# Hybrid four-mixer trunk: projection matmuls put in unbroken runs of 4096 columns

## The chip, the cores and the metric

The kernel runs on one core of one Trainium2 chip. The time is that of the device, from the start of the program to its end, in microseconds (us). PE is TensorE (PEld its weight loads), DVE VectorE, ACT ScalarE, POOL GpSimd, SP SyncE, from whose queue the DMAs here are issued.

## The reference

One decoder layer, float32, 2048 tokens of width 1024, then a final RMSNorm. One input projection (1024 to 9,232 columns) feeds four token mixers and their gates; each mixer's output goes through a SiLU gate path and its own projection, the four are merged by sigmoid gates, and one output projection closes the layer:

```python
h = rmsnorm(x, norm_g)
u = h @ w_in                       # split into the mixers' inputs, gate paths, merge gates
y_a = rg_lru(conv(lru_x)) * silu(lru_z)
y_b = (layernorm(sigmoid(m_o) * mlstm(q, k, v, i, f)) + skip * xm) * silu(m_z)
y_c = rmsnorm(gla(silu(h_q), hk, h_i, log_fh)) * silu(h_z)
y_d = rmsnorm(gla(g_q, g_k, g_v, log_gk)) * silu(g_z)
merged = sum(sigmoid(merge_n) * (y_n @ w_branch_n) for n in "abcd")
x = x + merged @ w_out
out = rmsnorm(x, final_g)
```

mLSTM, HGRN2 (`y_c`) and GLA (`y_d`) are recurrences over chunks of positions: within a chunk small products of queries, keys and values, between chunks a state that is decayed and added to.

## The kernel before

The sequence is worked in two halves of 1024 tokens, one after the other. Each half has these stages:

- **Ahead** (`ahead_pairs`, `ip_pair`): most of the input projection in seven products per pair of tiles (Strassen), with the LRU and the gate paths beside it. Its matmuls have line L423. 70 to 746 us and 1420 to 2097 us.
- **Mixers** (`mixers`): the mLSTM (`mlstm`, a generator), then four HGRN2 heads and two tiles with two GLA heads each, every one in two groups of 512 tokens (`gla_tile`, also a generator; 12 tiles per half). `both` steps the mLSTM beside the tiles. Between them stand projections that no mixer waits for at once: the values of the next heads (`ip_vals`, `ip_tok`, `tok_mm`: L280) and the last merge gates (`gate`, `ip_ch`, `proj_ch`: L268).
- **Merge** (`merge`): four branches of eight tiles, each tile two outputs of 512 tokens from 12 matmuls (`proj_ch`, L268). It starts while the last mixer tiles are still worked on; weights, gates and partial sums come and go by DMA.
- **Output** (`outp`): the output projection (`ip_tok`, `ip_tok_k`: L280) and the final norm.

Every projection is made of three matmuls per block of 128 inputs, since weights and activations are split into a high and a low part (`fp32r`): high by high, high by low, low by high. One output tile of `proj_ch` takes 24 matmuls of 512 columns (12 in the merge), one of `tok_mm` 24 of 256 or 264 columns. `wpieces` loads a block of weights (SP), casts it (ACT, L249) and forms the low part (POOL, L250). Projections write the PSUM banks `pb`, the recurrences the banks `mx`.

In a GLA tile, L997 and L1040 are the score products of 32 and 64 columns, at five levels; L1062 transposes the keys, L1068 forms the state's increments, which DVE turns into states at L1075, and L1083 and L1084 are the outputs. ACT squares and sums them (L1094), takes the logarithm and the exponential (L227, L1096) and scales them (L1102), PE transposes the result (L1106), and DVE multiplies it by the gate (L1107). In the mLSTM, L867 to L923 are its products and L945 a transpose. In the merge, ACT applies a tanh to the gates of the last two branches (L1313), and DVE multiplies by it out of PSUM (L1323); L1296 and L1297 split a branch's input.

The order on each engine is not written by hand. The framework's scheduler places instructions on all engines against a clock of its own; among those that are ready, the one with the smaller priority number goes first. Numbers count up in the order in which the code issues, and `prio(off)` lowers them for a block:

```python
p0 = tc.cur_priority
tc.cur_priority = max(0, p0 - off)
...
tc.cur_priority = p0 + (tc.cur_priority - s)
```

The mixers stand in `prio(MIX)` with `MIX = 4000`, evacuations and weight splits in `prio(EV)` with `EV = 6000`; the projections between them have no lowering. So a recurrence's matmul goes before a projection's as soon as it is ready, also in the middle of a projection's 24 matmuls. On the chip each engine keeps the order that the scheduler gave it.

Of the kernel before, what the change touches and what calls it, by code (L numbers as in the profile page):

```python
# [147 lines left out]
class Trunk:  # L148
# [90 lines left out]
    def wpieces(self, aps):  # L239
        nc = self.nc  # L240
        r = []
        with self.prio(self.EV):
            for ap in aps:
# [8 lines left out]
        return r  # L252

    EV = 6000

    def proj_ch(self, pieces, rh, rl, sink, ns=(0, 1)):


        nc = self.nc
        nk = 4 * len(pieces)  # L260
        for n in ns:
            ts = slice(n * 512, (n + 1) * 512)
            ps = self.pbank()
            for k in range(nk):
                hi, lo = pieces[k // 4]
                ws = slice((k % 4) * 128, (k % 4 + 1) * 128)
                for i, (w, h) in enumerate(((hi, rh[k]), (hi, rl[k]), (lo, rh[k]))):
                    nc.tensor.matmul(ps, w[:, ws], h[:, ts], start=(k == 0 and i == 0), stop=(k == nk - 1 and i == 2))  # L268
            sink(ts, ps)

    def ip_ch(self, name, j, sink, ns=(0, 1)):
# [3 lines left out]
    def tok_mm(self, v, c, k, pieces, ncol, first, last):  # L275
        hi, lo = pieces[k // 2]
        ws = slice((k % 2) * ncol, (k % 2 + 1) * ncol)
        cs = slice(c * 128, (c + 1) * 128)
        for i, (w, h) in enumerate(((hi, self.hh[k]), (lo, self.hh[k]), (hi, self.hl[k]))):
            self.nc.tensor.matmul(v, h[:, cs], w[:, ws], start=(first and i == 0), stop=(last and i == 2))  # L280

    def ip_tok(self, pieces, ncol, evac, single=8):

# [34 lines left out]
    def load_first(self, xs):  # L318
# [28 lines left out]
        for i, t in enumerate(tiles):  # L347
# [3 lines left out]
            def sink(ts, ps):  # L351
                with self.prio(self.EV):
                    V.tensor_tensor(th, ps, rb[:, :512], op=ALU.mult)
# [31 lines left out]
    def restore_block(self):  # L385

        nc = self.nc
        with self.prio(self.EV):
            for k in range(4):
# [10 lines left out]
    def ip_pair(self, t0, t1, fin, first=False):  # L400
# [4 lines left out]
        wc = self.a["wc"]  # L405
        with self.prio(self.EV):
            b11, b12, b22 = (r[:, :512] for r in self.wr)
# [4 lines left out]
        def product(x, w):  # L412
            with self.prio(self.EV):
                i = self.wi
                self.wi += 1
                hi, lo = self.wh[i % NW][:, :512], self.wl[i % NW][:, :512]
                A.activation(hi, w, AF.Copy)  # L417
                G.tensor_tensor(lo, w, hi, op=ALU.subtract)  # L418
            ps = self.bank8()
            for k, (xh, xl) in enumerate(self.op[x]):  # L420
                ws = slice(k * 128, (k + 1) * 128)
                for i, (wp, xp) in enumerate(((hi, xh), (hi, xl), (lo, xh))):
                    nc.tensor.matmul(ps, wp[:, ws], xp, start=(k == 0 and i == 0), stop=(k == 3 and i == 2))  # L423
            return ps

        def wsum(o, x, y):
            with self.prio(self.EV):
                V.tensor_tensor(o, x, y, op=ALU.subtract)  # L428
# [1124 lines left out]
```

## Time and profile before

| | us |
|---|---|
| median of 3 runs | 2724.45 (2722.39 to 2729.04) |
| the profiled execution | 2719.25 |
| its span, first to last instruction | 2717.4 |
| PE busy | 2596.0 |
| DVE, POOL, ACT busy | 1745.0, 1505.9, 1287.6 |

The profile shows one execution. Busy times are those of instructions on an engine, and a busy PE is not PE at its peak, since its matmuls overlap. "Clock" is the share of full speed that was granted to TensorE. A wait is idle time of an engine just before an instruction, put down to what ended it. In timelines, "x8" counts records, of which a float32 matmul has two and a transpose or an fp32r matmul one.

### The profile page before, as it was taken

How to read it: one execution, taken by the hardware profiler on the slowest of the kernel's cores; microseconds unless marked ns; L12 is line 12 of the kernel's file. 1: busy time of each engine (PE TensorE's matmuls, PEld its weight loads, DVE VectorE, ACT ScalarE, POOL GpSimd, SP SyncE). 2: the span in 40 equal slices, each digit the busy share in tenths (PEclk: the TensorE clock that was granted, in tenths of full speed). 3: DMA queues.
4: the chain of work that ended last, by engine and by line, in shares of the span. 5: the costliest groups of instructions: out<-in, count | busy, mean ns of one | idle time of the engine just before them, and what ended most of it. 6: DMA issues, size and time to landing. Idle time of an engine off the chain costs nothing. (4 is left out here: it accounts for less than half of the span.)

```text
span 2717.4 us, 45785 instructions
## 1 busy us (share of the span) xinstructions
PE 2596.0 (96%) x16800; PEld 2150.4 (79%) x16800; DVE 1745.0 (64%) x2907; ACT 1287.6 (47%) x2763; POOL 1505.9 (55%) x1273
## 2 busy tenths in 40 slices
PE   7999999999989998999999999999999999989999
PEld 5777878877878886778977777888787888767789
DVE  8787667447576778543375967764566677776342
ACT  5455444434454564443464454453345455644433
POOL 5566556444555555566475566554444555554763
PEclk8999999999999999999999999999999999999999
DMA  6233223443454336785442432233436533458821
GB/s 229 71 125 108 84 85 131 133 142 101 159 177 119 117 120 218 256 295 155 155 140 82 139 107 92 83 132 116 136 126 190 155 110 110 157 186 312 267 93 75
DMA packets 227072, 393.03 MB, mean 145 GB/s; under 512 B 20720, under 2 KB 78080, under 8 KB 226848
## 3 DMA queue, kind: packets, MB, share of 16 engines
q1 hardware_dynamic: 219360, 384.87, 42.9%
q10 hardware_dynamic: 7488, 5.24, 0.7%
q8 instruction: 132, 2.16, 0.3%
q14 instruction: 92, 0.75, 0.1%
HBM read 270.42 MB, written 119.60 MB: 144 GB/s over the span
## 5 line engine op out<-in xcount | busy, mean ns | idle before, releaser
L418 POOL TENSOR_TENSOR wl<-wr,wh 128x512 fp32r<-128x512 f32 x264 | 370.4, 1408 | 298.8 <-ACT wh L417 290.7
L418 POOL TENSOR_TENSOR wl<-gth,wh 128x512 fp32r<-128x512 f32 x198 | 286.9, 1449 | 280.1 <-ACT wh L417 268.6
L423 PE MATMUL mx<-s,wh 128*128 128x512 f32 x1248 | 394.0, 395 | 5.5 <-DVE arena L432 2.4
L432 DVE TENSOR_TENSOR arena<-arena,mx 128x512 f32<-128x512 f32 x386 | 252.3, 680 | 184.9 <-PE mx L423 168.3
L250 POOL TENSOR_TENSOR wl<-wr,wh 128x512 fp32r<-128x512 f32 (+1 forms) x176 | 249.1, 1423 | 179.3 <-ACT wh L249 144.9
L423 PE MATMUL mx<-hh,wl 128*128 128x512 f32 x824 | 328.6, 399 | 9.4 <-POOL wl L418 9.4
L423 PE MATMUL mx<-hh,wh 128*128 128x512 f32 x824 | 327.1, 397 | 5.6 <-DVE mqk L624 3.5
L423 PE MATMUL mx<-hl,wh 128*128 128x512 f32 x824 | 327.7, 398 | 2.3 <-DVE hl L306 2.3
L268 PE MATMUL pb<-hh,wh 128*128 128x512 f32 x704 | 289.2, 412 | 11.3 <-ACT hh L1296 3.4
L268 PE MATMUL pb<-hl,wh 128*128 128x512 f32 x704 | 287.2, 408 | 5.1 <-DVE hl L1297 5.1
L423 PEld LDWEIGHTS mx<-s,wh 128*128 128x128 f32 x1248 | 235.3, 189 | 62.4 <-DVE arena L432 2.8
L268 PE MATMUL pb<-hh,wl 128*128 128x512 f32 x704 | 284.1, 404 | 0.0
L417 ACT ACTIVATE wh<-wr 128x512 fp32r<-128x512 f32 x264 | 164.2, 627 | 227.3 <-PE mx L423 139.8
L280 PE MATMUL pb<-wh,hh 128*128 128x256 f32 (+1 forms) x880 | 255.3, 291 | 1.8 <-DVE lrt L1129 1.1
L280 PE MATMUL pb<-wl,hh 128*128 128x256 f32 (+1 forms) x880 | 254.5, 289 | 1.7 <-POOL wl L250 1.7
L280 PE MATMUL pb<-wh,hl 128*128 128x256 f32 (+1 forms) x880 | 253.5, 288 | 0.0
L423 PE MATMUL mx<-s,wl 128*128 128x512 f32 x624 | 245.0, 396 | 0.0
L417 ACT ACTIVATE wh<-gth 128x512 fp32r<-128x512 f32 x198 | 124.2, 627 | 228.9 <-DVE gth L428 185.5
L249 ACT ACTIVATE wh<-wr 128x512 fp32r<-128x512 f32 (+1 forms) x176 | 110.1, 629 | 187.1 <-PE pb L268 115.6
L423 PEld LDWEIGHTS mx<-hh,wl 128*128 128x128 f32 x824 | 156.2, 190 | 51.6 <-POOL wl L418 16.0
L423 PEld LDWEIGHTS mx<-hh,wh 128*128 128x128 f32 x824 | 156.5, 190 | 46.0 <-issue 6.9
L423 PEld LDWEIGHTS mx<-hl,wh 128*128 128x128 f32 x824 | 156.0, 189 | 41.0 <-DVE hl L306 3.5
(614 smaller groups left out, 6075.1 us busy)
## 6 DMA issues: line engine op xcount, KB each, us to landing
wr<-in_wc_dram SPq DMA_DIRECT2D x246, 256.0 KB, 2.7
g<-arena SPq DMA_DIRECT2D x52, 512.0 KB, 3.3
gth<-in_wc_dram SPq DMA_DIRECT2D x66, 256.0 KB, 2.8
wr<-in_wb_dram SPq DMA_DIRECT2D x64, 256.0 KB, 3.3
hl<-y SPq DMA_DIRECT2D x32, 512.0 KB, 5.8
arena<-g SPq DMA_DIRECT2D x48, 256.0 KB, 3.9
arena<-in_xT_dram SPq DMA_DIRECT2D x32, 256.0 KB, 4.7
lw<-g SPq DMA_DIRECT2D x32, 256.0 KB, 3.6
```

What stands on the lines that cost most here:

```text
L249: nc.scalar.activation(hi, raw, AF.Copy)
L250: nc.gpsimd.tensor_tensor(lo, raw, hi, op=ALU.subtract)
L268: nc.tensor.matmul(ps, w[:, ws], h[:, ts], start=(k == 0 and i == 0), stop=(k == nk - 1 and i == 2))
L280: self.nc.tensor.matmul(v, h[:, cs], w[:, ws], start=(first and i == 0), stop=(last and i == 2))
L417: A.activation(hi, w, AF.Copy)
L418: G.tensor_tensor(lo, w, hi, op=ALU.subtract)
L423: nc.tensor.matmul(ps, wp[:, ws], xp, start=(k == 0 and i == 0), stop=(k == 3 and i == 2))
L432: V.tensor_tensor(o, x, y, op=ALU.add)
```

## The change

Inside the loops of `proj_ch` and `tok_mm`, each matmul now stands in `run(i, n)`, with its number `i` in its output tile and its `n` columns. Where `i * n` is a multiple of 4096 the priority stays as it was; everywhere else it is lowered by 9000, more than the mixers' 4000. So the scheduler may put a recurrence's matmul ahead of a run's first matmul, and no longer ahead of the others: a run is 8 matmuls of 512 columns or 16 of 256. What is computed does not change.

```diff
--- before.py
+++ after.py
@@ -252,6 +252,16 @@
         return r
 
     EV = 6000
+    RUN = 9000
+
+    @contextmanager
+    def run(self, i, n):
+
+        if i * n % 4096:
+            with self.prio(self.RUN):
+                yield
+        else:
+            yield
 
     def proj_ch(self, pieces, rh, rl, sink, ns=(0, 1)):
 
@@ -265,7 +275,8 @@
                 hi, lo = pieces[k // 4]
                 ws = slice((k % 4) * 128, (k % 4 + 1) * 128)
                 for i, (w, h) in enumerate(((hi, rh[k]), (hi, rl[k]), (lo, rh[k]))):
-                    nc.tensor.matmul(ps, w[:, ws], h[:, ts], start=(k == 0 and i == 0), stop=(k == nk - 1 and i == 2))
+                    with self.run(3 * k + i, 512):
+                        nc.tensor.matmul(ps, w[:, ws], h[:, ts], start=(k == 0 and i == 0), stop=(k == nk - 1 and i == 2))
             sink(ts, ps)
 
     def ip_ch(self, name, j, sink, ns=(0, 1)):
@@ -277,7 +288,8 @@
         ws = slice((k % 2) * ncol, (k % 2 + 1) * ncol)
         cs = slice(c * 128, (c + 1) * 128)
         for i, (w, h) in enumerate(((hi, self.hh[k]), (lo, self.hh[k]), (hi, self.hl[k]))):
-            self.nc.tensor.matmul(v, h[:, cs], w[:, ws], start=(first and i == 0), stop=(last and i == 2))
+            with self.run(3 * k + i, 256):
+                self.nc.tensor.matmul(v, h[:, cs], w[:, ws], start=(first and i == 0), stop=(last and i == 2))
 
     def ip_tok(self, pieces, ncol, evac, single=8):
```

Lines behind the new method stand 12 further down in the changed kernel: L280 is L292, L945 is L957, L1040 is L1052, L1094 is L1106, L1102 is L1114, L1313 is L1325; L268 is L279.

Three places show what moves. The first is PE in the mixers, about the middle of the first half, where an mLSTM transpose (`mx_100<-cst`) and projections of values (`pb_98<-wh` and `wl`) meet. Before:

```order
L280 MATMUL pb_98<-wh_85,hh_67 128x264
L280 MATMUL pb_98<-wl_91,hh_67 128x264
L945 MATMUL mx_100<-cst,arena 128x128
L280 MATMUL pb_98<-wh_85,hl_75 128x264
L945 MATMUL mx_100<-cst,arena 128x128
L280 MATMUL pb_98<-wh_85,hh_68 128x264
L945 MATMUL mx_100<-cst,arena 128x128
L883 MATMUL mx_101<-mb_7_5093,mb_6_5092 128x128
L945 MATMUL mx_100<-cst,arena 128x128
L876 MATMUL mx_99<-mwv,mb_7_5093 128x128 x4
L883 MATMUL mx_101<-mb_7_5093,mb_6_5092 128x128 x3
L280 MATMUL pb_98<-wl_91,hh_68 128x264
```

With the change:

```order
L292 MATMUL pb_98<-wh_85,hl_75 128x264
L292 MATMUL pb_98<-wh_85,hh_68 128x264
L935 MATMUL mx_102<-mb_4_5090,arena 128x129 x2
L957 MATMUL mx_100<-cst,arena 128x128 x4
L888 MATMUL mx_99<-mwv,mb_7_5093 128x128 x4
L895 MATMUL mx_101<-mb_7_5093,mb_6_5092 128x128 x4
L292 MATMUL pb_98<-wl_91,hh_68 128x264
L292 MATMUL pb_98<-wh_85,hl_76 128x264
```

The four transposes stood one by one between projections; now they follow each other, and the projection's run is whole.

The second is PE beside the merge, at the score products of a late GLA tile (`mx_100` to `mx_103<-ma_0`). Before:

```order
L997 MATMUL mx_99<-arena 32x32 x16
L1040 MATMUL mx_100<-ma_0_5079 32x32 x8
L1040 MATMUL mx_101<-ma_0_5079 32x32 x8
L1040 MATMUL mx_102<-ma_0_5079 64x64 x4
L1040 MATMUL mx_103<-ma_0_5079 64x64 x4
L1062 MATMUL mx_104<-cst,arena 128x128 x4
L268 MATMUL pb_98<-hl_73,wh_85 128x512
```

With the change, up to the run that comes between them:

```order
L1052 MATMUL mx_100<-ma_0_5079 32x32 x8
L1052 MATMUL mx_101<-ma_0_5079 32x32 x8
L279 MATMUL pb_98<-hh_63,wh_87 128x512
L279 MATMUL pb_98<-hl_71,wh_87 128x512
L279 MATMUL pb_98<-hh_63,wl_93 128x512
L279 MATMUL pb_98<-hh_64,wh_87 128x512
```

The products of 32 columns and those of 64 followed each other directly. Now 20 merge matmuls (`pb_98`, `pb_97`), 48 score products of the next tile and 12 more merge matmuls stand between them.

The third is ACT at the end of the last GLA tile but one: sums of squares, logarithm, exponential, scalings (`ssq` are the sums) and the merge's first tanh. Before:

```order
L1094 ACTIVATE arena,ssq_203<-mx_101 128x128 x4
L227 ACTIVATE ssq_202<-ssq_202,small 128x4
L1018 ACTIVATE arena<-arena 128x512
L1054 ACTIVATE arena<-arena 128x512
L249 ACTIVATE wh_86<-wr_80 128x512
L227 ACTIVATE ssq_203<-ssq_203,small 128x4
L1096 ACTIVATE ssq_202<-ssq_202 128x4
L1313 ACT_TABLE_LOAD
L1313 ACTIVATE ma_0_5079<-ma_0_5079 128x512
L1096 ACTIVATE ssq_203<-ssq_203 128x4
L1102 ACTIVATE arena<-mx_100,ssq_202 128x128 x4
L1102 ACTIVATE arena<-mx_101,ssq_203 128x128 x4
```

With the change:

```order
L227 ACT_TABLE_LOAD
L227 ACTIVATE ssq_202<-ssq_202,small 128x4
L1106 ACTIVATE arena,ssq_203<-mx_101 128x128 x4
L1066 ACT_TABLE_LOAD
L1066 ACTIVATE arena<-arena 128x512
L1108 ACTIVATE ssq_202<-ssq_202 128x4
L227 ACT_TABLE_LOAD
L227 ACTIVATE ssq_203<-ssq_203,small 128x4
L1325 ACT_TABLE_LOAD
L1325 ACTIVATE ma_2_5081<-ma_2_5081 128x512
L1114 ACTIVATE arena<-mx_100,ssq_202 128x128 x4
L1108 ACTIVATE ssq_203<-ssq_203 128x4
```

The first tanh (`ma_0`) stood behind both logarithms. Now it stands ahead of them, a second one (`ma_2`) ahead of the scalings, and tables are loaded in between.

## Rows read from the trace of the kernel before

**Rows 1.** The page, part 1: busy us, share, instructions of each engine

```profile
PE 2596.0 (96%) x16800; PEld 2150.4 (79%) x16800; DVE 1745.0 (64%) x2907; ACT 1287.6 (47%) x2763; POOL 1505.9 (55%) x1273
```

**Rows 2.** Stretches: length, busy of PE, PEld, DVE, ACT, POOL; clock; DMA

```profile
746.00:1024.00 278.00, 255.12 (x2615) 231.90 (x2614) 205.63 (x497) 147.00 (x443) 154.53 (x166) 0.96 0.45 135
2097.00:2350.00 253.00, 233.23 (x2428) 213.39 (x2428) 187.29 (x455) 130.90 (x401) 137.95 (x148) 0.95 0.44 132
```

**Rows 3.** Waits of PE, 745 to 1200 us: total us, times, longest

```profile
PE mx L867 <- DMA mb<-pxm: 5.3, 1, 5.3
PE mx L997 <- DVE mb L1020: 3.4, 2, 2.4
PE mx L1084 <- DVE arena L1075: 3.4, 1, 3.4
...
PE mx L1062 <- DVE Cst L926: 2.2, 1, 2.2
```

**Rows 4.** Stretches of 1 us: at the first clock drop, and 900

```profile
810.00:811.00 1.00, 0.30 (x15) 0.18 (x14) 1.00 (x2) 1.00 (x2) 0.60 (x2) 1.00 0.58 211
811.00:812.00 1.00, 0.00 (x0) 0.00 (x0) 1.00 (x2) 0.04 (x1) 0.90 (x1) 0.96 0.17 59
812.00:813.00 1.00, 0.96 (x5) 0.74 (x5) 1.00 (x4) 0.00 (x0) 0.00 (x0) 0.50 0.60 221
815.00:816.00 1.00, 1.00 (x5) 0.77 (x5) 0.60 (x2) 0.43 (x2) 0.81 (x2) 0.83 0.98 238
900.00:901.00 1.00, 1.00 (x10) 1.00 (x10) 0.65 (x4) 0.00 (x0) 0.00 (x0) 1.00 0.00 0
```

**Rows 5.** Timeline of PE at 900 us: start, us, instruction

```profile
900.44 0.29 PE L280 MATMUL pb<-wl,hh 128*128 128x264 f32 x1
900.56 0.27 PE L1106 MATMUL mx<-cst,ma 128*128 128x128 f32 x1
900.59 0.37 PE L280 MATMUL pb<-wh,hl 128*128 128x264 f32 x1
900.79 0.27 PE L1106 MATMUL mx<-cst,ma 128*128 128x128 f32 x1
```

**Rows 6.** Timeline of PE beside the merge: matmuls behind waits, both halves

```profile
1043.37 0.45 PE L997 MATMUL mx<-arena 64*32 64x32 f32 x32 [2.92 <-ACT hh L1296]
...
1081.64 0.59 PE L997 MATMUL mx<-arena 64*32 64x32 f32 x27 [1.35 <-DVE ma L1107]
...
1120.08 0.66 PE L1040 MATMUL mx<-ma 64*64 64x64 f32 x4 [3.23 <-DVE arena L1023]
...
2388.79 0.63 PE L997 MATMUL mx<-arena 64*32 64x32 f32 x32 [2.91 <-ACT hh L1296]
...
2427.04 0.46 PE L997 MATMUL mx<-arena 64*32 64x32 f32 x32 [1.36 <-DVE ma L1107]
```

**Rows 7.** Stretches of 1 us in the two drops behind such waits

```profile
1120.00:1121.00 1.00, 0.92 (x12) 0.95 (x13) 1.00 (x4) 0.83 (x3) 0.34 (x1) 0.50 0.91 350
2430.00:2431.00 1.00, 1.00 (x8) 0.88 (x6) 1.00 (x3) 0.41 (x1) 0.94 (x2) 0.50 0.25 80
```

**Rows 8.** Line L1313: its table loads on ACT, ns min/median/max

```profile
L1313 ACT ACT_TABLE_LOAD  x2: 1283/1283/1283, 1144.1 to 2482.9; - x2
```

**Rows 9.** Timelines of ACT and PE at the last GLA tile but one

```profile
1139.36 0.28 ACT L1094 ACTIVATE arena<-mx 128x128 f32<-128x128 f32 x1 [4.05 <-PE mx L1084]
...
1146.01 2.15 ACT L1102 ACTIVATE arena<-mx,ssq 128x128 f32<-128x128 f32 x8
...
1147.43 0.40 PE L268 MATMUL pb<-hl,wh 128*128 128x512 f32 x1
1147.66 0.40 PE L268 MATMUL pb<-hh,wl 128*128 128x512 f32 x1
1147.90 0.49 PE L1106 MATMUL mx<-cst,arena 128*128 128x128 f32 x3
```

**Rows 10.** Groups of ACT by line: busy, mean ns, idle before, its end

```profile
L1313 ACT ACTIVATE arena<-arena 128x512 f32<-128x512 f32 x48 | 30.0, 630 | 49.8 <-DMA arena<-g 49.1
```

## The prediction

> **What bounds the kernel now.** I read the busy times first, then the stretches, then the waits of PE inside the stretch that the change touches, then single instructions. PE is the engine to look at: it is busy for 96% of the span [rows 1]. The Strassen stages (70 to 746 us and 1420 to 2097 us) contain none of the changed lines except at their edges. What the change reorders is the mixers and what is run beside them: 746 to about 1200 us and 2097 to about 2500 us. In the first 278 us of the mixers PE is busy for 255.1 us and its granted clock averages 0.96; in the second half of the sequence it is 233.2 of 253 us at 0.95 [rows 2]. So some 8% of this stretch is PE standing still, and a few per cent more is PE at half speed. Everything that the change can win lies there.
>
> PE stands still because it takes its instructions in the program's order, and comes to a matmul of a recurrence whose input DVE, ACT or a DMA has not finished [rows 3]. The clock follows. At 810 to 812 us PE has almost nothing to do, and from 812 the granted clock is 0.50, its lower level of 1.2 GHz; it is back at 2.4 GHz within the row of 815 [rows 4]. By those rows a drop takes 0.04 + 3 x 0.50 + 0.17 = 1.7 us of work from PE. There are 13 such drops in the two mixer stretches besides those at their starts (7 and 6; the first is this one, the last stands in [rows 7]), each right behind idle time of PE.
>
> **The change part by part.** It adds and removes no matmul and no DMA: PE has the same 14,038 instructions in the built program, SP the same 1,267 DMA issues, and the casts on ACT and subtractions on POOL that split the weights are as many as before. It moves PE instructions, and with them the order on the other engines. Five terms:
>
> *a. Start of the mixers.* PE waited 5.3 us for the first mLSTM operand [rows 3]. In the first half the order now has 16 projection matmuls ahead of that matmul instead of 5, in the second 24 instead of 19. At 0.12 us from one to the next [rows 5], 11 + 5 of them fill 1.9 us of standing time. **-1.9.**
>
> *b. Fewer changes of kind.* A single transpose between two projections costs more than itself: after it, the first projection takes 0.20 us (900.59 to 900.79) until the next instruction starts, where 0.12 is usual [rows 5], so an entry costs 0.08 us. Counted in the order, the recurrences break into the projections 99 and 98 times before the merge begins, now 53 and 52 times; in the merge 26 and 29 become 32 and 36. That is 79 fewer: **-6.3.** The Trainium skill (TensorE: Matmul & The Clock Gate, section "Architectural detail: the array is 16× 32×32, not 1× 128×128") says that PE's queue can pull weight loads ahead of matmuls in flight. By that rule an entry would cost nothing and this term would be 0. The trace disagrees, with its 0.08 us.
>
> *c. Waits in the middle.* A recurrence's matmul that gets ready during a run now stands behind what is left of it, half a run on average, 4 matmuls of 0.23 us [rows 9] or 8 of 0.12, about 0.9 us. Where PE used to wait for it, that time is now filled. PE's idle time in the middle is 22.9 us less the 5.3 of term a. The bounds are 0 and all 17.6 us per half. Near the lower end: the long waits are few (two for L1020, one each for L1075 and L926, 2.2 to 3.4 us [rows 3]), a run takes at most 0.9 from each, and projections fill only about half of the stretch. I take 3 us per half. **-6.**
>
> *d. Waits in the merge's part.* Here the order changes more, since the recurrences are down to their last tiles. Ahead of the L997 that waited 2.92 us, 36 more merge matmuls stand (8.3 us), 24 in the second half; ahead of the one that waited 1.35 us, 20 more (8 in the second half, 1.8 us, for 1.36); between the L1040 groups where 3.23 us were lost there were none, now 32 (7.4 us) [rows 6]. So 2.92 + 1.35 + 3.23 in the first half and 2.91 + 1.36 in the second should be covered: 11.8 us. Two clock drops right behind these waits go too [rows 7], 1.7 us each: 3.4. **-15.2.**
>
> *e. Table loads on ACT.* The merge's first tanh (L1313) now fall between the logarithms and exponentials of the last GLA tiles, and ACT has 41 table loads instead of 29, six more per half, each 1.28 us [rows 8]. In the last tile but one, four of them stand before the scalings that the transposes of L1106 need. Before, ACT took from 1139.36 to about 1147.1 for this (8 scalings end at 1148.2), and PE had matmuls until the transpose at 1147.90, 8.5 us of cover [rows 9]. Now ACT needs 7.7 + 4 x 1.28 = 12.8 us, and by the order (24 merge matmuls instead of 27) PE's cover is 7.8. PE stands 5.0 us, and behind the waiting transpose on PE are merge matmuls and the next tile's scores. In the last tile two loads stand between the two heads' scalings, while PE has the second head's first transpose straight behind the first head's: 2.6 us more. 7.6 per half: **+15.2.** The lower bound is 0, if the merge's transfers hold PE up there anyway (ACT already waited 49.1 us for gate tiles before L1313, [rows 10]); the upper adds one clock drop per half and such a wait of ACT, about 5 us per half.
>
> Sum: -1.9 - 6.3 - 6 - 15.2 + 15.2 = -14.2 us. The profiled execution took 2719.25 us (its span 2717.4), which is 5.2 below the median of the three runs, 2724.45. Against its own time the sum gives 2705.1; on the scale of the median **2710.3 us**, 0.5% less.
>
> **Rivals.** *A, slower: the recurrences become the bound.* In the third tile of each half the order now has 148 instructions of the recurrences in a row, without one projection; before, 61 projections stood among them, 7.3 us at 0.12. They have been moved ahead, so that the matmuls which feed DVE come 4 to 7 us later in PE's order just before this place. If DVE, ACT and POOL can't make that up, PE stands the whole 7.3 us there and the clock drops once more: 9.0 per half. It decides as soon as DVE's chain, not PE, sets the pace; the long waits for L1075 and L926 lie in this tile already [rows 3], which speaks for it. PE's 92% busy share there against DVE's 74% [rows 2] speaks against it. In place of term c: -14.2 + 6 + 18 = +9.8 for both halves, 2734 us; if the lateness is carried into the merge, so that d falls away too, 15.2 more.
>
> *B, no change: the waits only change places.* Covered at one matmul, they come back at the next, since the engines behind them are no faster. Terms c and d fall to 0, and half of e is covered: -1.9 - 6.3 + 7.6 = -0.6, 2724 us. For it: the same waits stand in both halves, so they are part of how the engines' speeds stand to each other.
>
> *C, faster: the runs keep the clock up.* If unbroken projections by themselves held it at 2.4 GHz, the other 11 drops would go as well: 18.7 us more, 2692 us. The Trainium skill (same page, section "🎯 Why this matters for your kernels") asks to avoid gaps between bursts of matmuls, since a gap brings the lower clock. The trace agrees about gaps. But it gives broken runs no blame: at 900 us projections alternate with single transposes [rows 5] and the clock reads 1.00 [rows 4].
>
> **How the numbers follow.** About 0.3% (8 us) can be told from no change. My forecast has 0.42: its own range is 2695 (e at 0) to 2718 (half of d missing), 0.34 of it faster and 0.08 the same. A has 0.22 (0.20 slower, 0.02 same), B 0.22 (0.02 faster, 0.14 same, 0.06 slower), C 0.14, all faster. Together faster 0.50, same 0.24, slower 0.26. The range 2686 to 2740 takes in B, A without its carry into the merge, and C's value; outside lie A's carry and cases in which several terms go the same way.
>
> **What would show it.** Right: the first wait at the mixers is near 4 us; PE's waits of 2.9 us and 3.2 us at L997 and L1040 in the merge are gone; new waits of several us stand at the transposes after the last two tiles, behind ACT table loads, of which ACT shows 41; PE's idle time from 746 to 1200 us is some 6 us less. Wrong: a wait of over 5 us in the third tile (A), an unchanged sum of idle time (B), or fewer than 8 clock drops with the same idle time (C).

## The result, and the profile after

The changed kernel takes 2743.71 us (median of 4 runs, 2736.75 to 2744.61) where the kernel before takes 2726.74 (2722.39 to 2729.68). The ratio is 1.0065, 95% interval 1.0048 to 1.0083: **0.65% slower**, some 17 us. The forecast was 2710.3 with a range up to 2740: wrong in sign, and outside the range.

The profiled execution is one of 2744.02 us, 24.8 more than that of before, which is itself 7.5 below its kernel's median: some 8 of the 24.8 are chance. The page, part 1, of the changed kernel answers to [rows 1]:

```profile
PE 2601.0 (95%) x16800; PEld 2156.8 (79%) x16800; DVE 1713.1 (62%) x2907; ACT 1304.5 (48%) x2775; POOL 1473.3 (54%) x1273
```

PE's busy time rose by 5.0 us with the same 16,800 records, beside a mean granted clock of 0.976 instead of 0.980; the span rose by 24.9 (2742.3 against 2717.4), so PE stood still 19.9 us longer. To see where, the matmuls of both traces were put at their places in PE's program order, and the work ahead of each was summed (0.23 us for 512 columns, 0.12 for 256, 0.05 to 0.24 for the recurrences'). The lag is the difference of the two times at which the same sum is reached. In us, changed kernel against before, by the places of before:

| stretch of PE's work | first half | second half | both |
|---|---|---|---|
| mixers up to the third tile (to 868 and 2214 us) | -5.2 | -4.1 | -9.3 |
| the third tile (to 905 and 2251) | +10.3 | +10.9 | +21.2 |
| the mixers' rest (to 1040 and 2385) | -3.2 | -3.1 | -6.3 |
| beside the merge (to 1149 and 2482) | -6.9 | -3.4 | -10.3 |
| the last two tiles (to 1224 and 2567) | +9.1 | +14.2 | +23.3 |
| the rest, and the Strassen stage between | +3.9 | +2.3 | +6.2 |

The weights are estimates, and others that fit as well move a row by some 2 us. Each trace is one execution, too. Four kernels of the experiments keep PE's order of before in the third tile (the three controls, and the one with the output's runs alone); their executions lag that of before there by 0.0 to 2.7 us in the first half and by 2.3 to 4.1 in the second. So some 4 of the 21.2 us belong to the execution of before.

By these rows the time was lost at two places per half, and won nearly everywhere else. The first is the third tile. It lies at 868 to 905 us and 2214 to 2251 us of the kernel before, in the columns of [rows 2]:

```profile
868.00:905.00 37.00, 33.83 (x354) 31.04 (x355) 30.20 (x85) 19.31 (x67) 18.99 (x24) 0.91 0.43 130
2214.00:2251.00 37.00, 34.56 (x361) 31.72 (x362) 30.29 (x85) 19.50 (x68) 18.00 (x24) 0.91 0.43 130
```

The same stretches of the changed kernel, and five single microseconds in the first:

```profile
868.00:905.00 37.00, 27.46 (x276) 24.26 (x274) 24.58 (x75) 18.36 (x65) 15.11 (x21) 0.82 0.35 104
2214.00:2251.00 37.00, 28.31 (x287) 25.27 (x286) 25.14 (x70) 17.93 (x54) 20.15 (x27) 0.82 0.42 126
...
875.00:876.00 1.00, 0.23 (x6) 0.05 (x8) 0.75 (x4) 0.97 (x5) 1.00 (x3) 1.00 0.43 154
879.00:880.00 1.00, 0.66 (x6) 0.47 (x5) 0.86 (x3) 0.70 (x3) 1.00 (x1) 0.78 1.02 292
880.00:881.00 1.00, 1.00 (x4) 0.82 (x4) 1.00 (x4) 0.91 (x5) 0.03 (x1) 0.50 0.95 222
...
885.00:886.00 1.00, 0.00 (x0) 0.00 (x0) 0.92 (x4) 0.00 (x0) 0.43 (x1) 0.50 0.91 249
892.00:893.00 1.00, 1.00 (x7) 1.00 (x6) 0.96 (x3) 0.00 (x0) 0.00 (x0) 0.50 0.00 0
```

PE is busy 6.4 us less, 6.3 in the second half, and the granted clock of the stretch is 0.82 instead of 0.91. The clock falls within the row of 879, behind several short waits of PE, the longest of 0.8 us, and is 0.50 from 880 to 893 us, through PE's gap at 883 to 887. DVE is busy less too, 24.6 us of 37. No engine sets the pace here. The waits of PE from 868 to 906 us of the changed kernel (total us, times, longest) are many, each for another link of the chain. The longest is for a load of the mLSTM that was issued at 881.15 us:

```profile
PE mx L879 <- DMA ma<-pxm: 4.0, 1, 4.0
PE pb L292 <- DVE lrt L1141: 2.2, 1, 2.2
PE mx L924 <- DVE arena L900: 1.1, 1, 1.1
PE mx L1009 <- DVE mb L930: 0.8, 1, 0.8
PE mx L1052 <- DVE mb L1032: 0.7, 1, 0.7
PE mx L1118 <- ACT arena L1114: 0.4, 1, 0.4
```

The second place is the end of the mixers. Waits of PE in the changed kernel, from 1145 to 1230 us, and from 2505 to 2570:

```profile
PE mx L1118 <- ACT arena L1114: 10.2, 3, 4.0
...
PE mx L1118 <- ACT arena L1114: 9.5, 3, 4.0
```

Before, PE did not wait for these scalings in either half. The timeline of ACT shows what it was doing ahead of the first of them (start, us, instruction), to be held against [rows 9], where the same work took ACT from 1139.36 to 1146.01:

```profile
1148.12 0.28 ACT L1106 ACTIVATE arena<-mx 128x128 f32<-128x128 f32 x1 [3.50 <-PE mx L1096]
...
1149.04 0.22 ACT L1106 ACTIVATION_READ_ACCUMULATOR arena<-mx 128x1 f32 x1
1149.27 1.28 ACT L1325 ACT_TABLE_LOAD   x1
1150.57 0.63 ACT L1325 ACTIVATE ma<-ma 128x512 f32<-128x512 f32 x1
...
1152.26 1.28 ACT L227 ACT_TABLE_LOAD   x1
...
1154.90 1.28 ACT L1066 ACT_TABLE_LOAD   x1
...
1156.94 1.28 ACT L227 ACT_TABLE_LOAD   x1
1158.23 0.30 ACT L227 ACTIVATE ssq<-ssq,small 128x4 f32<-128x4 f32 x1
1158.55 1.28 ACT L1325 ACT_TABLE_LOAD   x1
1159.84 0.63 ACT L1325 ACTIVATE ma<-ma 128x512 f32<-128x512 f32 x1
1160.38 1.12 ACT L1114 ACTIVATE arena<-mx,ssq 128x128 f32<-128x128 f32 x4
```

From the first square to the first scaling ACT needs 12.3 us instead of 6.7, and five loads of 1.28 us stand among it.

### The profile page after: what moved, and what is told of

Same layout as the page of the kernel before. It is cut to its first block, busy times and chain, and to the rows that moved or that the text cites. A ratio compares the mean times of both kernels' runs of the same rounds, so it can differ in the third digit from the quotient of the medians.

```text
span 2742.3 us, 45752 instructions
## 1 busy us (share of the span) xinstructions
PE 2601.0 (95%) x16800; PEld 2156.8 (79%) x16800; DVE 1713.1 (62%) x2907; ACT 1304.5 (48%) x2775; POOL 1473.3 (54%) x1273
## 4 chain that ended last, share of the span: by engine, by line
PE 71%; DVE 9%; DMA 6%; ACT 5%; POOL 5%; issue 3%; SPq 0%; POOLq 0%; DVEq 0%; ACTq 0%
PE mx L435 33%; PE pb L279 12%; PE pb L435 9%; PE pb L292 7%; POOL wl L430 1%; PE mx L1095 1%; PE mx L1096 1%; DMA ma<-pxm 1%; PE mx L1009 1%; POOL wl L250 1%; DMA ob<-in_x_dram 1%; DVE hl L318 1%; PE mx L879 1%; PE pb L799 1%; PE mx L1080 1%
## 5 line engine op out<-in xcount | busy, mean ns | idle before, releaser
L279 PE MATMUL pb<-hh,wh 128*128 128x512 f32 x704 | 289.6, 413 | 8.1 <-ACT gth L707 3.5
L279 PE MATMUL pb<-hh,wl 128*128 128x512 f32 x704 | 285.7, 407 | 0.0
L279 PE MATMUL pb<-hl,wh 128*128 128x512 f32 x704 | 285.4, 407 | 0.2 <-DVE hl L318 0.2
L292 PE MATMUL pb<-wl,hh 128*128 128x256 f32 (+1 forms) x880 | 254.8, 290 | 2.1 <-POOL wl L250 2.1
L292 PE MATMUL pb<-wh,hh 128*128 128x256 f32 (+1 forms) x880 | 250.6, 286 | 3.8 <-DVE lrt L1141 2.2
L292 PE MATMUL pb<-wh,hl 128*128 128x256 f32 (+1 forms) x880 | 248.8, 283 | 1.1 <-DVE hl L1347 1.1
```

## The experiments

The ratios are against runs of the kernel before on the same chip, with 95% intervals. Two theories stood first: **T**, the table loads on ACT made the loss; **A**, the third tile made it.

**Hold the tanh back.** The merge's tanh gets an order behind the last scaling (`self.scaled`), in the changed kernel and, as a control, in the kernel before:

```diff
-                    A.activation(o[:, cc], po[:, cc], AF.Copy, scale=ss[:, c:c + 1])
+                    self.scaled = A.activation(o[:, cc], po[:, cc], AF.Copy, scale=ss[:, c:c + 1])
...
-                        A.activation(t[:, :512], t[:, :512], AF.Tanh, scale=0.5)
+                        self.after(A.activation(t[:, :512], t[:, :512], AF.Tanh, scale=0.5), self.scaled)
```

> The changed kernel with one more order: the merge's tanh (L1325) on ACT may not pass the last scaling (L1114) of the last GLA tile. ACT has 25 table loads in the built program instead of 41; the recurrences' 148 instructions in a row in the third tile stay. Theory T (the loss of 17 us is made by the table loads between the logarithms and scalings of the last two GLA tiles, term e of the prediction, which was too small): the waits of PE at L1118 behind L1114 (3.95, 2.63 and 3.57 us in the first half, 3.96, 1.79 and 3.72 in the second, 19.6 together) go, with a clock drop or two: 2718 to 2726 us, where the changed kernel has 2744. Theory A (the recurrences bound in the third tile, where the changed kernel falls back by some 10 us per half against the kernel before): the time stays at 2738 to 2746 us, since the third tile is as it was.

> Control: the kernel before with the same hold of the tanh behind the last scaling; 25 table loads instead of 29, no runs. Both theories: the order of PE is nearly that of before and PE did not wait there, so the time is that of before, 2724 to 2729 us. If it gains 5 us or more, what the hold gives to the changed kernel is not only the undoing of a harm that the change did.

Measured: 2740.05 us, 1.0041 (1.0029 to 1.0054), and the control 2722.28, 0.9981 (0.9968 to 0.9995), 1.7 us below what was expected of it. Against its control the change still costs 0.6%. Taken alone this speaks for A. But the hold made a wait of its own. Waits of PE from 1145 to 1230 us in the changed kernel with the hold:

```profile
PE mx L1118 <- ACT arena L1114: 3.2, 1, 3.2
PE pb L279 <- DVE ma L1335: 2.2, 1, 2.2
```

The merge's multiplications (L1335) need the tanh, so the merge's matmuls stood behind it too. In PE's order the last tile's transposes now follow its last output matmul directly, where 16 merge matmuls lie between them in the change and 24 before. The last tiles' lag against before is some +8 and +17 us, no better than in the changed kernel. The run doesn't tell T from A.

**Runs in one kind of projection alone.** In `tok_mm` the run is taken away, in the next kernel that of `proj_ch` instead, with the hold:

```diff
-            with self.run(3 * k + i, 256):
-                self.nc.tensor.matmul(v, h[:, cs], w[:, ws], start=(first and i == 0), stop=(last and i == 2))
+            self.nc.tensor.matmul(v, h[:, cs], w[:, ws], start=(first and i == 0), stop=(last and i == 2))
```

> Runs in proj_ch alone; the matmuls of tok_mm keep their priority. The built program has no stretch of 148 recurrence instructions in the third tile (the projections stand among them as before), and 41 table loads on ACT as in the changed kernel. Theory T: the loss stays, 2738 to 2748 us, with waits of 10 us or more per half at the transposes L1118 (here L1117). Theory A: the loss is gone, 2720 to 2729 us.

> Runs in tok_mm alone, and the tanh held behind the last scaling: the third tile has 156 recurrence instructions in a row, ACT 25 table loads, and the merge's matmuls are not in runs. Theory A: slower than before by 10 to 20 us, 2737 to 2747. Theory T: within 5 us of before, 2722 to 2732, since what the third tile loses (some 10 us per half in the changed kernel) is what was won ahead of it and is won behind it (some 5 and 4 us).

Measured: with `proj_ch` alone 2723.52 us, 0.9993 (0.9983 to 1.0004); with `tok_mm` alone and the hold 2748.52, 1.0081 (1.0068 to 1.0094). The first is A's number, the second a little above it. That the first has all 41 table loads and is no slower than before seemed to rule T out; it doesn't, as the runs below show.

**No tanh.** The tanh becomes a copy, in both kernels, so that the gates are left unsquashed. In each PE keeps its order, instruction for instruction:

```diff
-                        A.activation(t[:, :512], t[:, :512], AF.Tanh, scale=0.5)
+                        A.activation(t[:, :512], t[:, :512], AF.Copy, scale=0.5)
```

> The changed kernel with the merge's tanh (L1325) replaced by a scaled copy on the same engine and of the same size, so the gates of the last branches are not squashed: what it leaves out is that function. ACT has 23 table loads instead of 41; PE's order is that of the changed kernel, instruction for instruction. Theory T (table loads): the waits at L1118 in the last two tiles (19.6 us) go, 2720 to 2728 us. Theory A (the recurrences uncovered in the third tile): that tile falls back by 10 us per half as before; the last tiles give at most 8 us, 2736 to 2744 us.

> Control: the kernel before with the same copy in place of the tanh; 23 table loads instead of 29, PE's order unchanged. Both theories: 2720 to 2728 us, since PE does not wait for these loads before the change. The difference to the run with the changed kernel without tanh is what the change costs apart from table loads: under 4 us by theory T, 12 to 20 us by theory A.

Measured: 2725.49 us, 0.9993 (0.9974 to 1.0013), and the control 2724.13, 0.9991 (0.9974 to 1.0009). T's numbers: 18 us come back with the table loads, and 2 in the control too, whose interval includes no change. The timeline of ACT at the same place, without the loads:

```profile
1146.04 0.28 ACT L1106 ACTIVATE arena<-mx 128x128 f32<-128x128 f32 x1 [3.50 <-PE mx L1096]
...
1151.74 0.63 ACT L1325 ACTIVATE ma<-ma 128x512 f32<-128x512 f32 x1 [4.56 <-DMA ma<-g]
...
1155.31 0.63 ACT L1325 ACTIVATE ma<-ma 128x512 f32<-128x512 f32 x1
1155.83 1.14 ACT L1114 ACTIVATE arena<-mx,ssq 128x128 f32<-128x128 f32 x4
```

The scaling still comes 9.8 us after the first square, 4.6 of them behind a gate tile's DMA, and PE waits for none of them any more. The third tile falls back by 9.7 and 9.3 us in this kernel as well, so what A names is there, and it is paid for by gains elsewhere.

**Which runs of `tok_mm`.** They are 256 columns wide for the HGRN2 values and the output projection, 264 for the GLA values. Without the former (the diff), and with the former alone, none in `proj_ch`:

```diff
-            with self.run(3 * k + i, 256):
+            with self.run(3 * k + i if ncol == 264 else 0, 256):
```

> The changed kernel without runs in the 256-column products of tok_mm (the values of the HGRN2 heads); the 264-column ones and proj_ch keep theirs. The longest stretch of recurrence instructions in the third tile falls from 148 to 64, the tail of the mixers has the changed kernel's order and ACT its 41 table loads. Theory A: the 10 us per half of the third tile come back, of which 4 to 5 per half had been won ahead of it: 2724 to 2734 us. Theory T: 2740 to 2748 us.

> Runs in the 256-column products of tok_mm alone. The third tile has 156 recurrence instructions in a row, the tail of the mixers the cover of before (24 merge matmuls ahead of its transposes), ACT 31 table loads. Theory A: the whole loss or more, 2738 to 2750 us. Theory T: 2724 to 2732 us. If it is the runs of 264 columns that made the kernel with runs in tok_mm alone slow (2748.5), this one is at 2725 to 2732 too.

Measured: 2735.55 us, 1.0036 (1.0020 to 1.0051), between the two expectations, and 2747.22, 1.0069 (1.0044 to 1.0094), A's. The stretch 868 to 905 us in the kernel without runs of 256 columns:

```profile
868.00:905.00 37.00, 32.68 (x348) 29.87 (x348) 32.33 (x80) 19.73 (x69) 21.07 (x26) 0.91 0.44 130
```

And in the one that has these alone:

```profile
868.00:905.00 37.00, 26.45 (x257) 23.08 (x258) 28.66 (x78) 17.57 (x58) 17.21 (x25) 0.77 0.37 111
```

PE's busy time in the third tile goes with the runs of 256 columns. Its clock does not go with them alone: in the kernel with the output's runs alone (below), whose order there is that of before, it is 0.86 and 0.77.

The first kernel still has all 41 table loads. So has the one with `proj_ch` alone, which is 12 us faster by the ratios; their runs differ by the 264 columns. Waits of PE for the scalings from 1145 to 1230 us, in the kernel with `proj_ch` alone and in the one without runs of 256 columns:

```profile
PE mx L1117 <- ACT arena L1113: 2.4, 1, 2.4
...
PE mx L1118 <- ACT arena L1114: 8.8, 3, 4.0
```

The second half adds 2.4 and 8.3, so it is 4.8 against 17.1 us, about the difference of the two. With `proj_ch` alone the first scaling comes 8.9 us after the first square (1143.57 to 1152.45), with four loads between them, and 28 merge matmuls stand ahead of the last tile's transposes; the other kernel has there the 16 of the change. The number of loads does not set the price: it depends on where they fall, and on what PE has to do meanwhile.

**Neither loss.** Runs in `proj_ch` alone and no tanh; then three kernels in which the gates of the third branch are formed without leaving the table of exp and ln, and the tanh of the fourth branch is held back:

```diff
-                        A.activation(t[:, :512], t[:, :512], AF.Tanh, scale=0.5)
+                        if ni == 2:
+                            A.activation(t[:, :512], t[:, :512], AF.Exp, scale=-1.0)
+                            self.ln(t[:, :512], t[:, :512], bias=1.0)
+                            self.gate2 = A.activation(t[:, :512], t[:, :512], AF.Exp, scale=-1.0)
+                        else:
+                            i = A.activation(t[:, :512], t[:, :512], AF.Tanh, scale=0.5)
+                            self.after(i, self.scaled)
+                            self.after(i, self.gate2)
...
-                        V.scalar_tensor_tensor(th[:, :512], th[:, :512], 1.0, ps, op0=ALU.add, op1=ALU.mult)
+                        if ni == 2:
+                            V.scalar_tensor_tensor(th[:, :512], ps, 2.0, th[:, :512], op0=ALU.mult, op1=ALU.mult)
+                        else:
+                            V.scalar_tensor_tensor(th[:, :512], th[:, :512], 1.0, ps, op0=ALU.add, op1=ALU.mult)
```

> Runs in proj_ch alone and the copy in place of the merge's tanh (what it leaves out is that function): neither the long row of recurrences in the third tile nor the extra table loads (23 of them). Theory S (three terms that add: the table loads cost 18 us, by the 2744 with and 2725.5 without them; the runs in tok_mm cost 20, by 2747 with the 256-column ones alone; so the runs in proj_ch must win some 20): 2702 to 2710 us. Theory R (they do not add, and the runs in proj_ch win no more than the 3 us that the kernel with them alone showed): 2717 to 2725 us.

> The same with nothing left out: runs in proj_ch alone, and the gates of the third branch as exp(-ln(1 + exp(-x))) on ACT, whose functions need no other table, the tanh of the fourth branch behind the last scaling. 25 table loads in the built program. ACT has 32 more activations of 512 columns per half (0.63 us each) beside the merge. Theory S: 2704 to 2716 us, the fastest so far. Theory R: 2717 to 2728 us.

> The changed kernel, all its runs, with the same gates of the third branch: 25 table loads instead of 41, nothing left out. Theory T and S: the 18 us come back as in the kernel without tanh, 2722 to 2730 us. If it stays at 2738 or more, the gain of the kernel without tanh was not that of the table loads alone.

> Control: the kernel before with the same gates of the third branch, no runs, 25 table loads instead of 29. 2721 to 2728 us by every theory; what it gains is to be taken from the gains of the two others.

| kernel | us | ratio to before |
|---|---|---|
| runs in `proj_ch`, no tanh | 2711.18 | 0.9931 (0.9919 to 0.9944) |
| runs in `proj_ch`, exp and ln | 2714.18 | 0.9944 (0.9931 to 0.9958) |
| all runs, exp and ln | 2730.16 | 1.0004 (0.9994 to 1.0014) |
| before, exp and ln | 2719.76 | 0.9962 (0.9949 to 0.9975) |

The three with runs are within 1.2 us of what theory S gave, and none is in R's range; the control is 1.2 us below what was expected. Without both losses the runs in `proj_ch` win 0.6% (0.9931 against the control's 0.9991). The whole computation with exp and ln is **0.56% faster than before** and 1.2% faster than the change. Waits of PE from 1145 to 1230 us in it:

```profile
PE pb L279 <- DVE arena L1342: 3.9, 1, 3.9
```

No transpose waits for ACT any more. Of its 0.56%, 0.38 are the gates' own by the control, so its runs win 0.2% here, within the intervals, and 0.6% without tanh. The control's order on PE differs from before as well (36 merge matmuls ahead of the last transposes, not 24), so the two are not the same comparison; the difference stays open.

The same holds for the price of the loads. Against its control the change as a whole costs 0.02% without tanh (0.9993 against 0.9991), but 0.42% with exp and ln (1.0004 against 0.9962) and 0.6% with the tanh held back. Only without tanh does PE keep its order in both kernels, so that pair prices the loads alone; in the two others most of the loss stands although the added loads are gone, and why is not shown. The two losses do not simply add up.

**Where `tok_mm` loses.** The output projection goes through `tok_mm` too. `self.mixing` is set where the mixers begin and cleared where the output stage does. The diff is that of the kernel with the runs of the HGRN2 values alone; the condition is `not self.mixing` for the output's alone (both without runs in `proj_ch`), and `self.mixing` for all but the output's:

```diff
-            with self.run(3 * k + i, 256):
+            with self.run(3 * k + i if self.mixing and ncol == 256 else 0, 256):
```

> Runs only where tok_mm is called by the output stage. The mixers have PE's order of before, ACT 29 table loads. Theory V (the loss is made in the third tile): 2724 to 2730 us, within 4 us of before. Theory O (a good part is made in the output, 4 to 5 us at the end of the first half's and 1 to 2 in the second's): 2730 to 2734 us.

> Runs only in the 256-column products of the HGRN2 values in the mixers: 156 recurrence instructions in a row in the third tile, output as before, 31 table loads. Theory V: 2740 to 2748 us, as with all runs of 256 columns (2747). Theory O: 2735 to 2742 us, some 6 less than those.

> All runs of the change but those in the output stage: 41 table loads, third tile with 148 in a row. Theory V: 2740 to 2746 us, as the changed kernel (2744). Theory O: 2736 to 2740 us.

Measured: the output's runs alone 2726.02 us, 1.0005 (0.9990 to 1.0020); the values' alone 2743.20, 1.0073 (1.0055 to 1.0090); all but the output's 2737.07, 1.0050 (1.0033 to 1.0066). The first two are theory V's numbers, the third is O's. The values' runs alone cost as much as the whole change, and the output's alone nothing: the loss is made by the runs in the mixers. The stretch 868 to 905 us in the kernel with these alone:

```profile
868.00:905.00 37.00, 25.70 (x268) 23.02 (x267) 24.87 (x72) 18.70 (x66) 14.75 (x20) 0.84 0.34 101
```

Its third tiles lose 14 to 16 us each by the lag; beside the merge of the first half 8 of them come back, in the second none. Taking the output's runs out of the change gives 0.15% back, within the intervals of the two.

## Why the prediction was wrong

**Terms a, b and c** were -14.2 together. The stretches of the mixers that they speak of, apart from the third tile, came 15.6 us earlier (9.3 + 6.3). That the sums are alike is luck. Of term a nothing is left by 764 us: the first wait fell from 5.3 to 3.4 us, as forecast, but one of 1.3 us follows it, and the lag there is 0.2. Term b is a misreading. Eight transposes in a row, before:

```profile
1147.90 1.03 PE L1106 MATMUL mx<-cst,arena 128*128 128x128 f32 x8
```

One takes 0.27 us, so they start 0.11 apart ((1.03 - 0.27) / 7). In [rows 5] a transpose and the projection behind it take 0.23 together (900.56 to 900.79), which is that 0.11 and the usual 0.12: the projection starts only 0.03 after the transpose, and its 0.20 makes up for it. An entry costs nothing there, so b should have been 0, and the trace did not speak against the rule cited with it. What came is, by exclusion, what c is about, waits filled by work from further on; it is not measured apart, and it was paid for in the third tile.

**Rival A** is the step that failed: the forecast put the third tile at nothing. A named the tile, the 148 instructions in a row and 9.0 us per half; measured were 10.3 and 10.9. But it was given 0.22, and put *in place of* term c, where it came on top of it: 21.2 us. The argument against it was "PE's 92% busy share there against DVE's 74%". These are means over 278 us. In a tile without projections the recurrences need no busy engine to be slow: PE waits in turn for DVE, for ACT and for a load of the mLSTM, while DVE is busy for 24.6 us of 37. "It decides as soon as DVE's chain, not PE, sets the pace" was the wrong condition; it decides as soon as PE has nothing to do between the links of the chain. The projections that had filled these gaps now stand ahead of the tile. There they win something (the kernel with the values' runs alone gains some 8 and 2 to 4 us up to this tile), and cost more in the tile (14 to 16 each). The price of the clock was too small as well: one drop was taken at 1.7 us, but the clock stayed at 0.50 from 880 to 893 us. By rows of 1 us PE was busy for 9.0 of these 13, so this one cost some 4.5; the stretch as a whole lost less by it, since it had 0.91 before, not 1.00. The Trainium skill (TensorE: Matmul & The Clock Gate, section "🎯 Why this matters for your kernels") warns of gaps between matmuls; the trace agrees that the clock fell behind idle time of PE, but the waits just ahead of the fall were of 0.8 us and less, and the gap at 883 to 887 us came when it was low already. The sign that was to show A, a wait of over 5 us in the tile, did not come: the longest is 4.0, and the loss is the sum of many. Nor did PE's idle time from 746 to 1200 us fall by some 6 us; it went from 37.6 to 36.7.

By the experiments the `tok_mm` runs cost 0.6 to 0.7% in the whole, 16 to 20 us: the ratios are 1.0065 with and 0.9993 without them, 0.9993 against 0.9931 without tanh, 1.0004 against 0.9944 with exp and ln. In the first pair most of that can be PE's waits for the scalings, which are 19.7 and 4.8 us; in the second neither kernel has any in those stretches, so it is this pair that speaks for the tile.

**Term d** was -15.2, of which -10.3 came. The waits of 3.23, 2.92 and 1.35 us [rows 6] are gone, as forecast, but one of 2.5 us came at another L997 (L1009 now, behind DVE's L992). The first half won 6.9 us of 9.2, the second 3.4 of 6.0.

**Term e** had the right mechanism and a wrong size. Forecast were waits of 5.0 us in the last tile but one and 2.6 in the last; measured 3.95 and 6.2 (2.63 + 3.57) in the first half. With the second half's 3.96 and 5.5 that makes 19.6, where 15.2 was forecast. Clock drops came with these waits, which the forecast kept for its upper bound: the clock is 0.50 in the rows of 1160, 1208, 2519 and 2563 us. By the kernel without tanh the loads cost 16 to 18 us of the time (18.2 less the control's 2), by the two other pairs less. For ACT in the last tile but one the forecast was 12.8 us to the end of the first four scalings; it took 13.4 (1148.12 to 1161.50). The last tile was the mis-sized one, with 6.2 and 5.5 us for 2.6, and with it the sum of e.

**Not priced** was the rest, 6.2 us, mostly at the output's end of the first half (+5.2 from 1382 to 1432 us). The kernel with the output's runs alone falls back there too (+5.3), the one without them does not (-0.2); but the former's whole time is that of before, so a part must be won elsewhere. PE's order is not quite the same there: some 40 of its 180 records from 1382 to 1432 us have other places. PE's waits behind ACT (L707) and POOL (L318) from 1375 to 1435 us are 3.5 us each, where they were 1.5 and 1.6 before. Which of these is the cause stays open.

**Rival B** describes the mixers without the last tiles, 15.6 us won and 21.2 lost; but the waits came back where projections were missing, not at the next instruction. **Rival C** fell: the mean clock from 746 to 1024 us stayed at 0.96.

So the sum by the rows is -15.6 + 21.2 - 10.3 + 23.3 + 6.2 = +24.8 us for the profiled executions, of which the medians show 17. With A at its own 18 on top of term c, not in its place, the forecast would have been 3.8 us above before; the rest is d, e and what wasn't priced.

## What to carry to other kernels

Independent matmuls that fill the gaps of a recurrence are a stock: an order that spends them earlier wins there and loses where they are missing, so look for the longest stretch of the dependent chain that is left without any, and price it as bare latency, with the clock that it brings down. A mean of busy shares over the stage does not tell it. When matmuls move on PE, read the order of ACT too: activations of different tables that come to alternate cost a load each (1.28 us here), on a path that nobody touched. Count the loads, but price them by where they fall and by the work that PE has meanwhile.

## What was not expected of the hardware

A switch of tables cost 1.30 us from the end of one activation to the start of the next: the last square's sum ends at 1149.26, and with the load of 1.28 at 1149.27 the tanh begins at 1150.57. The Trainium skill (ScalarE: Activation LUTs, section "What ACT_TABLE_LOAD costs") gives 1.28 us for the load and 1.38 more to drain, 2.66 in all. The load's 1.28 us agrees; the 1.38 do not show in these rows. By 2.66 a switch, an estimate from that figure, the five in this tile would have been 13.3 us of ACT, more than the 12.3 that all of it took.
